# Eleven modulation chunks of a two-layer decoder trunk, moved from the expert loops into the second layer's mixing

## The chip, the cores and the metric

The kernel runs on one core of a Trainium2 chip. The metric is the time of one execution on the device in microseconds, the median of several runs. One execution was also taken by the hardware profiler. The engines are PE (matrix products), DVE and ACT (element-wise work), POOL and SP; besides their arithmetic, POOL, SP and ACT issue DMAs. Weights come from device memory (HBM) in chunks of 128 x 1024 float32, 512 KB, into on-chip memory (128 partitions).

## What is computed

A trunk of two layers over 256 tokens of width 1024. Each layer has a token mixing (convolution, windowed attention, spatial gating) and a retrieval of experts by product keys. Six modulation vectors of each layer, from one conditioning vector, shift and scale both inputs and gate both outputs:

```python
c_act = jax.nn.silu(c)
mod = (c_act @ w_ada + b_ada)[:, None, :]
sh1, sc1, g1, sh2, sc2, g2 = jnp.split(mod, 6, axis=-1)
h = rms_norm(x, norm1_g) * (1 + sc1) + sh1
proj = h @ w_in
...
x = x + g1 * (merged @ w_out)
h2 = rms_norm(x, norm2_g) * (1 + sc2) + sh2
x = x + g2 * peer_ffn(h2, peer_wq, peer_sub_keys, peer_down, peer_up)
```

In `peer_ffn` each token has 8 heads; each head takes the best 16 of 128 x 128 experts by the sum of two key scores. An expert is one row of `peer_down` (dot with h2, then gelu, times a softmax gate) and one row of `peer_up` (added with that weight).

## The kernel before

**Experts.** The first 168 tokens of layer 0 and the first 160 of layer 1 are computed densely over all 16384 experts, in two loops of 128 tiles, 128 experts each. The *down loop* (L1234 to L1329) multiplies a 512 KB tile of `peer_down` with the tokens on PE (`chunk_mm`, L357), and from some tile on makes the gates of four tokens with eight small matmuls (`gate_mm`, L1133), from one-hots that DVE compares (L1107) and ACT scales (L1117 to L1123). The gated activations `acts` fill the low part of an arena of on-chip memory, tile by tile. The *up loop* (`combine`, L1173) multiplies them with tiles of `peer_up` and adds up in PSUM.

The other 88 or 96 tokens are computed by *gathered rows*. POOL fetches 128 expert rows by an indirect DMA of 512 KB (`fetch`, L1074). DVE makes dots of the rows of `peer_down` (`dot`, L1084, in the down loop) and adds the rows of `peer_up` (`add_row`, L1099, in the up loop). PE folds the sums into PSUM at tile 125 of the up loop (`folds`, L1179). A dot or an add sets its buffer free, and only then does POOL fetch another row into it. Buffers are fixed places of the arena: among them those of early down tiles that have been used (`AHEAD_AT`).

**The picks.** The top-k work of the two token blocks on DVE is a list of pieces with costs (`fills`). Block 1 goes first, then block 0; `run_fill` runs pieces within a budget a tile. When a block's pieces are done, three transposes on PE (L934, two tiles later) bring its picks into place. Rows can be fetched from three tiles after block 1 is done (tile `begin`: 11 in layer 0, 12 in layer 1). Gates begin some tiles after both blocks' transposes. Until block 0 is done, `DOT_SLOW` dots are due in a tile; from `start` on it is `DOT_RATE`.

**The stream of chunks.** `Src.seq` lists all chunks in the order of use. Dense tiles, through a ring of 7 buffers, go alternately by ACT's and by SP's DMA queue. The *asides*, 48 chunks of `w_ada` that make the second layer's modulation, stand in the list between the tiles, at places in `ASIDES_AT` for the down loops and spread over tiles 4 to 100 of layer 0's up loop (`ASIDES_UP`). They go by SP's queue into six buffers of their own, and DVE multiplies each with `cact` and sums it (L227). The rows have POOL's queue. Each queue is served in order.

**Where the order comes from.** The expert loops run in the order in which they are written, with the decisions above taken when the program is built. The instructions of the mixing and of the other stages are ordered by a scheduler; each engine takes its own in that order. The *bridge* (L424) joins a layer's end to the next mixing: updates of X on DVE (L392), its squares' sums, the reciprocal `rn` (L376), the scaled input (L481, L487). In the mixing, chunks of `w_in` and `w_out` are split into two halves (ACT L277, DVE L270) and multiplied in three products (L359 to L361), beside attention (L606 logits, L611 to L626 softmax on DVE).

Of the kernel before, what the change touches and what calls it, by code (L numbers as in the profile page):

```python
# [14 lines left out]
OP = mybir.AluOpType  # L15
# [4 lines left out]
S = 256  # L20
DC = 8
D = 1024
# [24 lines left out]
WHERE_LAG = 3  # L47
SETS_LAG = 6
SETS_KNOWN = 22
D_FIRST = 8  # L50
DOT_SLOW = 0.3
DOT_RATE = (0.85, 0.92)
DOT_FAST = 1.6
RETIRE = 9
AHEAD_AT = (8, 12, 16, 36, 40, 44, 48, 52, 56, 60, 64, 68, 100, 28, 32)
KEPT = 100
FLUSH = 6
FIRST_LOWER = 1
AHEAD_FIRST = 4
ASIDES_AT = ((20,) * 6 + tuple(range(46, 125, 5)), (20,) * 6 + (60, 72))  # L60
ASIDES_UP = (4, 100)
F_FIRST = 4
F_LAST = 124
HELD = 2
FILL = 1.5
FILL_DOWN = (2.2, 2.1)
# [16 lines left out]
def hybrid_trunk(ctx: ExitStack, tc: tile.TileContext, x_in, c_in, vec_in, w_ada, w_in, w_out, w_pq,  # L83
# [118 lines left out]
    def dma_ahead(upto):  # L202
        while Src.loaded < min(upto, len(Src.seq)):
            kind, src, raw = Src.seq[Src.loaded]
            if kind == "aside":
                raw = stream.tile([P, D], F32, name="aside", tag=("hi", "lo")[Src.aside % 2], bufs=3)
                Src.aside += 1
            elif kind != "early":
                raw = stream.tile([P, D], F32, name="raw", tag="raw", bufs=RAW)
            if kind == "second":  # L210
                Src.later.append((Src.loaded, raw, src))
            else:
                nc.sync.dma_start(raw, src)
            raws[Src.loaded] = raw
            Src.loaded += 1
# [32 lines left out]
    def cast_step(late=None):  # L248
        k = Src.cast
        if k >= len(Src.seq):  # L250
            return False
        dma_ahead(k + 1)
        while Src.later and Src.ring[Src.later[0][0]] <= Src.ring[k + 1] - 1 + RAW - QUEUE_LAG:
            nc.scalar.dma_start(*Src.later.pop(0)[1:])
        kind, _, arg = Src.seq[k]
        raw = raws.pop(k)
        Src.cast += 1
        if kind == "aside":
            Src.asides.append((k, lambda: ada_chunk(arg[0], arg[1], raw)))
        elif kind == "ada":  # L260
            ada_chunk(arg[0], arg[1], raw)
        elif kind in ("whole", "early", "second"):
            ready.append((raw, None))
        else:
            hi = stream.tile([P, D], F32R, name="hi", tag="hi", bufs=3)
            lo = stream.tile([P, D], F32R, name="lo", tag="lo", bufs=3)

            def low():
                if arg is None:
                    nc.vector.tensor_sub(lo, raw, hi.bitcast(F32))  # L270
                else:
                    nc.vector.scalar_tensor_tensor(lo, raw, arg, hi.bitcast(F32), op0=OP.mult,
                                                   op1=OP.subtract)

            with tc.high_priority(offset=AHEAD):
                if arg is None:
                    nc.scalar.copy(hi, raw)  # L277
                else:
                    nc.scalar.activation(hi, raw, AF.Copy, scale=arg)
                if late is None:  # L280
                    low()
                else:
                    late.append(low)
            ready.append((hi, lo))
        load_more(k)
        return True
# [16 lines left out]
    def ada(layer, groups, kind="ada"):  # L303
        return [(kind, w_ada[layer, p], (layer, p)) for g in groups for p in range(8 * g, 8 * g + 8)]
# [11 lines left out]
    def mats(src, layer, n, kind="mat"):  # L316
        return [(kind, src[layer, p], None) for p in range(n)]

    seq = []
    for layer in range(DEPTH):  # L320
        body = [("whole" if n in WHOLE_IN[layer] else "mat", w_in[layer, n], None) for n in range(16)]
# [2 lines left out]
        if layer == 0:  # L324
# [6 lines left out]
            body = head + body[n:]  # L331
            body = first[:2] + body[:n] + first[2:] + mix(body[n:], ada(0, [2, 3, 4]))
        body += mix(tail[:6], ada(0, [5])) + tail[6:] if layer == 0 else tail
        seq += body + [("whole" if n in WHOLE_PQ else "mat", w_pq[layer, n], None) for n in range(16)]
        dn, un = ([t if n % 2 else ("second", *t[1:]) for n, t in enumerate(mats(w, layer, 128, "whole"))]
                  for w in (down, up))
        for n, at in enumerate(AHEAD_AT):
            dn[AHEAD_FIRST + n] = ("early", dn[AHEAD_FIRST + n][1], region(at * S, D))
        aside = ada(1, [0, 1, 2, 3, 4] if layer + 1 < DEPTH else [5], "aside")
        for n, at in reversed(tuple(enumerate(ASIDES_AT[layer]))):  # L340
            dn.insert(at, aside[n])
        if layer + 1 < DEPTH:
# [3 lines left out]
    Src.seq = seq  # L346
    for t in seq:
        Src.ring.append(Src.ring[-1] + was if Src.ring else 0)
        was = t[0] not in ("early", "aside")
    Src.ring.append(Src.ring[-1] + was)  # L350
    dma_ahead(RAW)

# [655 lines left out]
    def experts(layer, rest):  # L1008
# [225 lines left out]
        for i in range(128):  # L1234
# [32 lines left out]
                known_to[0] = SETS[0][1]  # L1267
                fetch()
            if start is None:
                run_fill(FILL_DOWN[layer] if begin is None else FILL_DOWN[layer] - 1.2 * DOT_SLOW)  # L1270
            if known:
                known_at.append((i + PICKS_LAG, known.pop()))
                if begin is None:
# [25 lines left out]
                for row in [row for row in free if any(row is r for r in passing)]:  # L1299
                    free.remove(row)  # L1300
            n = i - AHEAD_FIRST
            if 0 <= n < len(AHEAD_AT) and AHEAD_AT[n] >= 28:
                assert not retired
                free.append(region(AHEAD_AT[n] * S, D))
                if AHEAD_AT[n] != KEPT:
                    passing.append(free[-1])
                fetch()
# [130 lines left out]
```

## Time and profile before

| | us |
|---|---|
| median of 3 runs | 1582.73 (1582.06 to 1584.29) |
| profiled execution | 1584.51, span 1582.6 |
| layer 0: mixing and queries | 0 to 188.85 |
| layer 0: down loop, up loop | 188.85 to 509.46, to 823.6 |
| layer 1: mixing and queries | 823.6 to 976.9 |
| layer 1: down loop, up loop | 976.9 to 1285.8, to the end |

The stages' borders are read from PE's timeline. In the rows that follow, an instruction is named by engine and line, with output and inputs. A bracket such as `[3.54 <-DMA raw<-in_up]` is the time for which the engine stood before it, and what ended that. A group's row has its count, busy time and mean, then idle time and what ended most of it. `raw` is the ring of dense tiles, `arena` the big on-chip memory in which row buffers lie too, `spots` the dots' inputs, the sums and three more row buffers.

### The profile page before, as it was taken

The numbers are of one execution on the slowest core, as the hardware profiler recorded it, in microseconds if no ns is written. First come the engines' busy times: TensorE is split into PE (matmuls) and PEld (weight loads), VectorE is DVE, ScalarE is ACT, GpSimd is POOL, SyncE is SP. The second block draws the span as 40 slices with busy tenths as digits, with TensorE's granted clock in tenths as the row PEclk, the third lists the DMA queues.
The fourth block names the chain that finished last, engine by engine and source line by source line (L and its number), as shares of the span: only waits on it lengthen the run. The fifth ranks groups of instructions, "written<-read, shape, count | busy, mean of one in ns | idle before, by whom it ended". The sixth has DMA issues, their size and how long they took to land.

```text
span 1582.6 us, 28957 instructions
## 1 busy us (share of the span) xinstructions
PE 1542.3 (97%) x11240; PEld 1505.1 (95%) x11240; DVE 1000.0 (63%) x2255; ACT 472.5 (30%) x1356; POOL 496.8 (31%) x424
## 2 busy tenths in 40 slices
PE   6999999999999999998999999999999999999997
PEld 5879999999999999998999899999999999999997
DVE  6778898677787444444337578877667754444434
ACT  2346313465553000000026663134656610000000
POOL 1000124334344434444200001245443334444441
PEclk9999999999999999999999999999999999999998
DMA  9998489999999999999955574899999999999995
GB/s 385 339 375 319 138 289 348 418 418 419 417 418 416 415 419 419 418 419 419 412 189 171 186 258 139 292 351 419 417 418 419 418 419 419 418 419 419 419 418 211
DMA packets 156681, 571.21 MB, mean 361 GB/s; under 512 B 18131, under 2 KB 18659, under 8 KB 155392
## 3 DMA queue, kind: packets, MB, share of 16 engines
q1 hardware_dynamic: 66096, 241.07, 39.7%
q0 software_dynamic: 55744, 202.36, 32.0%
q10 hardware_dynamic: 34704, 125.93, 19.9%
q8 instruction: 88, 1.44, 0.3%
q14 instruction: 49, 0.40, 0.1%
HBM read 564.02 MB, written 4.09 MB: 359 GB/s over the span
## 4 chain that ended last, share of the span: by engine, by line
PE 40%; DMA 38%; issue 8%; DVE 7%; POOL 4%; ACT 2%; ACTq 0%; POOLq 0%; SPq 0%; DVEq 0%
DMA arena<-in_up,arena 17%; PE acc L1173 17%; DMA arena<-in_down_rows,arena 12%; PE ch L357 9%; DMA spots<-in_down_rows,arena 3%; DMA raw<-in_up 3%; POOL arena L1074 3%; PE ch L359 2%; PE ch L360 2%; PE ch L361 2%; DVE raw L227 1%; DMA raw<-in_w_ada 1%; PE ch L446 1%; DVE arena L1084 1%; PE g L952 1%
## 5 line engine op out<-in xcount | busy, mean ns | idle before, releaser
L1173 PE MATMUL acc<-arena,raw 128*128 128x168 f32 (+1 forms) x4096 | 580.5, 305 | 9.0 <-DMA raw<-in_up 9.0
L1173 PEld LDWEIGHTS acc<-arena,raw 128*128 128x128 f32 x4096 | 577.6, 192 | 11.3 <-DMA raw<-in_up 11.2
L357 PE MATMUL ch<-arena,raw 128*128 128x168 f32 (+2 forms) x3776 | 560.7, 307 | 0.1
L357 PEld LDWEIGHTS ch<-arena,raw 128*128 128x128 f32 x3776 | 536.2, 190 | 5.6 <-issue 1.8
L1099 DVE SCALAR_TENSOR_TENSOR spots<-arena,spots 128x1024 f32<-128x1024 f32 x156 | 200.4, 1284 | 222.1 <-DMA arena<-in_up,arena 220.8
L1074 POOL DMA_INDIRECT arena<-in_up,arena x159 | 215.1, 1353 | 280.5 <-DMA arena<-in_up,arena 203.9
L1074 POOL DMA_INDIRECT arena<-in_down_rows,arena x151 | 178.3, 1181 | 242.9 <-DVE arena L1084 180.7
L1084 DVE SCALAR_TENSOR_TENSOR arena<-arena,spots 128x1024 f32<-128x1024 f32 x151 | 183.1, 1222 | 86.1 <-DMA arena<-in_down_rows,arena 79.6
L1117 ACT ACTIVATE arena<-arena,parts 128x128 f16<-128x128 f16 x164 | 64.6, 394 | 142.1 <-DVE arena L1107 102.5
L388 ACT ACT_TABLE_LOAD x6 | 7.7, 1283 | 284.9 <-PE acc L1173 284.8
L357 PE MATMUL ch<-arena 128*128 128x160 f32 (+2 forms) x544 | 86.0, 317 | 6.1 <-issue 3.6
L357 PEld LDWEIGHTS ch<-arena 128*128 128x128 f32 x544 | 79.8, 192 | 11.2 <-ACT arena L410 5.2
L1150 ACT ACTIVATE arena<-ch 128x336 f32<-128x336 f32 (+32 forms) x122 | 41.9, 343 | 149.4 <-PE ch L357 128.9
L227 DVE SCALAR_TENSOR_TENSOR aside<-aside,arena 128x1024 f32<-128x1024 f32 x48 | 58.6, 1220 | 43.9 <-DMA aside<-in_w_ada 43.8
L359 PE MATMUL ch<-hh,hi 128*128 128x256 f32 x288 | 82.6, 289 | 2.0 <-DVE arena L477 1.9
L360 PE MATMUL ch<-hh,lo 128*128 128x256 f32 x288 | 81.8, 284 | 0.0
L361 PE MATMUL ch<-hh,hi 128*128 128x256 f32 x288 | 81.7, 284 | 0.0
L270 DVE TENSOR_TENSOR lo<-raw,hi 128x1024 fp32r<-128x1024 f32 x42 | 51.2, 1225 | 37.3 <-ACT hi L277 36.3
L227 DVE SCALAR_TENSOR_TENSOR raw<-raw,arena 128x1024 f32<-128x1024 f32 x48 | 57.9, 1217 | 8.9 <-DMA raw<-in_w_ada 5.4
L1119 ACT ACTIVATE arena<-arena,parts 128x128 f16<-128x128 f16 x164 | 63.4, 387 | 0.0
L1123 ACT ACTIVATE arena<-arena,parts 128x128 f16<-128x128 f16 x164 | 63.4, 386 | 0.0
L1121 ACT ACTIVATE arena<-arena,parts 128x128 f16<-128x128 f16 x164 | 63.4, 386 | 0.0
(231 smaller groups left out, 1661.9 us busy)
## 6 DMA issues: line engine op xcount, KB each, us to landing
raw<-in_up SPq DMA_DIRECT2D x128, 512.0 KB
raw<-in_up ACTq DMA_DIRECT2D x128, 512.0 KB
raw<-in_down SPq DMA_DIRECT2D x114, 512.0 KB
raw<-in_down ACTq DMA_DIRECT2D x112, 512.0 KB
raw<-in_w_ada SPq DMA_DIRECT2D x48, 512.0 KB
aside<-in_w_ada SPq DMA_DIRECT2D x48, 512.0 KB
raw<-in_w_pq SPq DMA_DIRECT2D x32, 512.0 KB
arena<-in_down SPq DMA_DIRECT2D x30, 512.0 KB
```

Source lines behind the costliest of these rows:

```text
L227: nc.vector.scalar_tensor_tensor(raw, raw, 1.0, cact, op0=OP.mult, op1=OP.mult, accum_out=mods[layer][:, col:col + 1])
L357: nc.tensor.matmul(dst, hi[:, cols], k[0], start=start, stop=stop, **kw)
L359: nc.tensor.matmul(dst, hi[:, cols], k[0], start=start, stop=False, **kw)
L360: nc.tensor.matmul(dst, lo[:, cols], k[0], start=False, stop=False, **kw)
L361: nc.tensor.matmul(dst, hi[:, cols], k[1], start=False, stop=stop, **kw)
L1074: nc.gpsimd.indirect_dma_start(out=held[n], out_offset=None, in_=rows if n >= TS else down_rows[:, :], in_offset=bass.IndirectOffsetOnAxis ...
L1084: nc.vector.scalar_tensor_tensor(row, row, 1.0, R_DX[which(k)[0]], op0=OP.mult, op1=OP.mult, accum_out=R_DOTS[:, k:k + 1])
L1099: nc.vector.scalar_tensor_tensor(R_SUM[s], row, w, R_SUM[s], op0=OP.mult, op1=OP.add)
L1117: nc.scalar.activation(og[0][:, 0, i, :], oh[:, 0, i, :], AF.Copy, scale=parts[:, 0, t + i:t + i + 1])
L1119: nc.scalar.activation(og[1][:, 0, i, :], oh[:, 0, i, :], AF.Copy, scale=parts[:, 1, t + i:t + i + 1])
L1121: nc.scalar.activation(og[0][:, 1, i, :], oh[:, 1, i, :], AF.Copy, scale=parts[:, 0, t + 2 + i:t + 3 + i])
L1173: nc.tensor.matmul(acc[d // 2][:, (d % 2) * S:(d % 2) * S + T], u[:, d * P:(d + 1) * P], acts[:, i, :], start=i == 0 and d % 2 == 0, stop= ...
```

## The change

The 11 chunks are columns 24 to 31 (the second layer's second shift, `sh2`) and 40 to 42 (of its last gate, `g2`). They are no asides any more. A new kind of chunk, `inline`, loads them by POOL's DMA queue into named places of the arena, and DVE multiplies them there:

```diff
+MIXED = ((24, 10, 76), (25, 10, 80), (26, 10, 84), (27, 11, 29), (28, 11, 33), (29, 11, 37), (30, 11, 41), (31, 14, 17), (40, 19, 45), (41, 20, 49), (42, 22, 17))
...
-            if kind == "aside":
+            if kind == "inline":
+                raw = raw[0]
+                nc.gpsimd.dma_start(raw, src)
+            elif kind == "aside":
...
+        if kind == "inline":
+            view = (lambda v: v.rearrange("p (a b) -> p a b", a=2)) if len(raw.shape) == 3 else (lambda v: v)
+            nc.vector.scalar_tensor_tensor(raw, raw, 1.0, view(cact), op0=OP.mult, op1=OP.mult,
+                                           accum_out=mods[arg[1]][:, arg[2]:arg[2] + 1])
+            ada_end(arg[1], arg[2], 8)
...
+    def beside(layer, n):
+        return [mixed(col, at) for col, m, at in MIXED if layer == 1 and m == n]
...
+        body = [t for n, b in enumerate(body) for t in [b] + beside(layer, n)]
...
+        aside = [t for t in aside if t[2][1] not in apart]
```

Each entry is a column, the chunk of the second mixing's list behind which it stands, and a place in units of 256 columns. The asides left are 18 in layer 0's down loop (22 before), 14 in its up loop (18), and 5 in layer 1's down loop (8). With this go the pace of the dots, the row buffers and the picks' budget:

```diff
-D_FIRST = 8
-DOT_SLOW = 0.3
+D_FIRST = 7
+DOT_SLOW = 0.9
...
-RETIRE = 9
+RETIRE = 4
...
-ASIDES_AT = ((20,) * 6 + tuple(range(46, 125, 5)), (20,) * 6 + (60, 72))
+ASIDES_AT = ((20,) * 6 + tuple(range(46, 125, 7)), (20,) * 5)
...
-                run_fill(FILL_DOWN[layer] if begin is None else FILL_DOWN[layer] - 1.2 * DOT_SLOW)
+                if begin is None or i < begin + D_FIRST:
+                    run_fill(FILL_DOWN[layer])
+                elif fills[0]:
+                    run_fill(FILL_DOWN[layer] - 1.2 * DOT_SLOW)
+                else:
+                    run_aside()
...
-            if 0 <= n < len(AHEAD_AT) and AHEAD_AT[n] >= 28:
+            if 0 <= n < len(AHEAD_AT) and AHEAD_AT[n] >= 36:
```

`D_FIRST` is the tile after `begin` from which dots are due. `RETIRE` is the number of pieces left at which the passing row buffers are given up. The last line takes two places (28 and 32) from the row buffers.

How the order moves is shown at three places. The first is the end of the picks in layer 1's down loop. On PE, L357 (L379 of the changed kernel) is the dense tiles' matmul, eight a tile, and L934 (L956) the transposes of the picks; L1133 (L1155) is the first gate. Before:

```order
L1035 MATMUL g<-ident,arena 96x128 x8
L357 MATMUL ch<-arena,raw 128x160 x8
L357 MATMUL ch<-arena 128x160 x88
L934 MATMUL g<-ident,arena 128x128 x3
L357 MATMUL ch<-arena 128x160 x32
L357 MATMUL ch<-arena,raw 128x160 x128
L934 MATMUL g<-ident,arena 128x128 x3
L357 MATMUL ch<-arena,raw 128x160 x64
L1133 LDWEIGHTS arena
```

and in the changed kernel:

```order
L1057 MATMUL g<-ident,arena 96x128 x8
L379 MATMUL ch<-arena,raw 128x160 x8
L379 MATMUL ch<-arena 128x160 x88
L956 MATMUL g<-ident,arena 128x128 x3
L379 MATMUL ch<-arena 128x160 x32
L379 MATMUL ch<-arena,raw 128x160 x184
L956 MATMUL g<-ident,arena 128x128 x3
L379 MATMUL ch<-arena,raw 128x160 x72
L1155 LDWEIGHTS arena
```

The second transposes stand behind 7 more tiles (184 - 128 = 56 matmuls), at tile 41 for 34, and the first gate one tile more, at 50 for 42. In layer 0 the same count moves the second transposes from tile 32 to 38. On DVE at that place, L1084 (L1106) is a dot, L902 to L912 (L924 to L934) match picks, L922 to L924 (L944 to L946) make the softmax gate that the transposes need. Before:

```order
L902 TENSOR_TENSOR arena<-arena,iota_87 128x2048
L907 TENSOR_TENSOR arena<-arena 128x2048
L911 TENSOR_TENSOR arena<-arena 128x8x128
L911 TENSOR_TENSOR arena<-arena 128x8x64
L911 TENSOR_TENSOR arena<-arena 128x8x32
L912 TENSOR_TENSOR arena<-arena 128x128
L1084 SCALAR_TENSOR_TENSOR arena<-arena,spots 128x1024
L922 TENSOR_REDUCE arena<-arena 128x8
L923 RECIPROCAL arena<-arena 128x8
L924 TENSOR_TENSOR arena<-arena 128x128
L1084 SCALAR_TENSOR_TENSOR arena<-arena,spots 128x1024 x3
```

and in the changed kernel:

```order
L929 TENSOR_TENSOR arena<-arena 128x2048
L1106 SCALAR_TENSOR_TENSOR spots,arena<-spots 128x1024
L1106 SCALAR_TENSOR_TENSOR arena<-arena,spots 128x1024
L933 TENSOR_TENSOR arena<-arena 128x8x128
L933 TENSOR_TENSOR arena<-arena 128x8x64
L933 TENSOR_TENSOR arena<-arena 128x8x32
L934 TENSOR_TENSOR arena<-arena 128x128
L1106 SCALAR_TENSOR_TENSOR arena<-arena,spots 128x1024 x2
L944 TENSOR_REDUCE arena<-arena 128x8
L945 RECIPROCAL arena<-arena 128x8
L946 TENSOR_TENSOR arena<-arena 128x128
L1106 SCALAR_TENSOR_TENSOR arena<-arena,spots 128x1024
```

Dots stand between the pieces: 18 ahead of the gate in layer 1 now (3 before), 16 in layer 0.

The second place is DVE's part of the bridge from layer 0 to layer 1's mixing; L264 of the changed kernel is an inline chunk's product. Before:

```order
L270 TENSOR_TENSOR lo<-raw,hi 128x1024
L392 SCALAR_TENSOR_TENSOR arena<-acc,mod_111,arena 128x256 x8
L439 TENSOR_TENSOR arena<-arena 128x256 x2
L442 TENSOR_TENSOR arena<-arena 128x256 x6
L270 TENSOR_TENSOR lo<-raw,hi 128x1024
L376 RECIPROCAL rn<-rn 128x2
L481 TENSOR_TENSOR arena<-arena,g 128x512 x2
L487 SCALAR_TENSOR_TENSOR hh<-arena,mod_112,hh 128x256 x2
```

and in the changed kernel:

```order
L264 SCALAR_TENSOR_TENSOR arena,mod_112<-arena 128x1024
L279 TENSOR_TENSOR lo<-raw,hi 128x1024
L414 SCALAR_TENSOR_TENSOR arena<-acc,mod_111,arena 128x256 x8
L461 TENSOR_TENSOR arena<-arena 128x256 x2
L464 TENSOR_TENSOR arena<-arena 128x256 x6
L279 TENSOR_TENSOR lo<-raw,hi 128x1024
L264 SCALAR_TENSOR_TENSOR arena,mod_112<-arena 128x1024
L398 RECIPROCAL rn<-rn 128x2
L264 SCALAR_TENSOR_TENSOR arena,mod_112<-arena 128x1024
L503 TENSOR_TENSOR arena<-arena,g 128x512 x2
```

The products of columns 24, 25 and 26 stand before the updates, before the reciprocal, and before the scaling of the input. The third place is POOL's queue in layer 0's up loop, where L1096 is a fetched row and L208 an inline chunk's load; in the changed kernel it reads:

```order
L1096 DMA arena<-in_up,arena 128x1024 x6
L208 DMA arena<-in_w_ada 128x1024
L1096 DMA arena<-in_up,arena 128x1024 x3
L1096 DMA spots<-in_up,arena 128x1024
L1096 DMA arena<-in_up,arena 128x1024 x2
L208 DMA arena<-in_w_ada 128x1024
L1096 DMA arena<-in_up,arena 128x1024 x7
```

Columns 27 and 28 are loaded behind the 50th and the 56th row, where before rows alone stood; the other nine loads come behind the loop's last row. The products of these two stand on DVE behind the 46th and 47th add.

More of the change, by code (lines that the diff above doesn't have):

```diff
@@ L211, in dma_ahead @@
                 Src.later.append((Src.loaded, raw, src))
-            else:
+            elif kind != "inline":
                 nc.sync.dma_start(raw, src)
@@ L257, in cast_step @@
         Src.cast += 1
-        if kind == "aside":
+        if kind == "inline":
[3 more added lines that the diff above has]
+            ada_end(arg[1], arg[2], 8)
+        elif kind == "aside":
             Src.asides.append((k, lambda: ada_chunk(arg[0], arg[1], raw)))
@@ L317, in mats, with mixed @@
         return [(kind, src[layer, p], None) for p in range(n)]
+    def mixed(col, at):
+        if at == 90:
+            raw = region(at * S, 2 * D).rearrange("p (a b) -> p a b", a=2)[:, :, :D // 2]
+        else:
+            raw = region(at * S, D)
+        return ("inline", w_ada[1, col], (raw, 1, col))
+    def beside(layer, n):
+        return [mixed(col, at) for col, m, at in MIXED if layer == 1 and m == n]
+    apart = [col for col, _, _ in MIXED]
     seq = []
@@ L348, in hybrid_trunk @@
         Src.ring.append(Src.ring[-1] + was if Src.ring else 0)
-        was = t[0] not in ("early", "aside")
+        was = t[0] not in ("early", "aside", "inline")
     Src.ring.append(Src.ring[-1] + was)
@@ L1269, in experts @@
             if start is None:
-                run_fill(FILL_DOWN[layer] if begin is None else FILL_DOWN[layer] - 1.2 * DOT_SLOW)
+                if begin is None or i < begin + D_FIRST:
+                    run_fill(FILL_DOWN[layer])
+                elif fills[0]:
+                    run_fill(FILL_DOWN[layer] - 1.2 * DOT_SLOW)
+                else:
+                    run_aside()
             if known:
```

## The prediction

> **What bounds the kernel now.** I read the page's head and its slices first, then the busy time by stage, then the waits of PE and of DVE in the stages that the change touches. From the page:
>
> ```profile
> span 1582.6 us, 28957 instructions
> PE 1542.3 (97%) x11240; PEld 1505.1 (95%) x11240; DVE 1000.0 (63%) x2255; ACT 472.5 (30%) x1356; POOL 496.8 (31%) x424
> ...
> L1173 PE MATMUL acc<-arena,raw 128*128 128x168 f32 (+1 forms) x4096 | 580.5, 305 | 9.0 <-DMA raw<-in_up 9.0
> ...
> L1084 DVE SCALAR_TENSOR_TENSOR arena<-arena,spots 128x1024 f32<-128x1024 f32 x151 | 183.1, 1222 | 86.1 <-DMA arena<-in_down_rows,arena 79.6
> ```
>
> PE is busy 97% of the span, so only PE's waits, its slow clock, and work that pushes it back can move the end. The stages, from the windows table (stretch; busy us and instructions of PE, PEld, DVE, ACT, POOL; granted clock; DMA share; GB/s):
>
> ```profile
> 188.85:268.70 79.85, 78.14 (x549) 77.43 (x548) 68.16 (x319) 15.99 (x30) 28.21 (x32) 1.00 0.84 292
> 509.46:674.00 164.54, 164.53 (x1154) 164.06 (x1153) 79.80 (x78) 0.45 (x1) 68.45 (x53) 1.00 1.03 418
> 674.00:787.00 113.00, 104.68 (x704) 103.37 (x703) 48.52 (x47) 0.00 (x0) 41.32 (x32) 0.97 1.03 419
> 823.60:880.00 56.40, 56.31 (x436) 54.15 (x436) 42.11 (x91) 37.88 (x90) 0.00 (x0) 1.00 0.58 187
> 1057.40:1285.80 228.40, 226.23 (x1814) 223.18 (x1813) 165.52 (x313) 125.67 (x450) 94.49 (x85) 0.99 1.03 418
> 1285.80:1560.00 274.20, 273.52 (x2011) 273.04 (x2011) 119.06 (x97) 0.72 (x2) 125.12 (x90) 1.00 1.02 417
> ```
>
> The row at 509.46 is the first part of layer 0's up loop, that at 674 its end; 823.6 to 880 is the start of layer 1's mixing; the last two are layer 1's down loop after its picks, and its up loop. In the expert loops the DMA engines are full at 418 GB/s; in the mixing they are not (187). A chunk of 512 KB costs 524288 B / 418 GB/s = 1.254 us of a full DMA. PE loses time to that only at the end of layer 0's up loop. Its rows there in the timeline (start, us, wait in brackets), the chain's last full-speed stretch before, and the windows table at the largest wait:
>
> ```profile
> 682.17 9.39 PE L1173 MATMUL acc<-arena,raw 128*128 128x168 f32 x64 [1.03 <-DMA raw<-in_up]
> 692.11 8.11 PE L1173 MATMUL acc<-arena,raw 128*128 128x168 f32 x55 [0.56 <-DMA raw<-in_up]
> ...
> 734.75 8.78 PE L1173 MATMUL acc<-arena,raw 128*128 128x168 f32 x48 [3.54 <-DMA raw<-in_up]
> 744.26 4.83 PE L1173 MATMUL acc<-arena,raw 128*128 128x168 f32 x32 [0.73 <-DMA raw<-in_up]
> 751.54 18.76 PE L1173 MATMUL acc<-arena,raw 128*128 128x168 f32 x118 [2.46 <-DMA raw<-in_up]
> ...
> 509.63 157.55 PE acc L1173 x1104
> ...
> 730.00:740.00 10.00, 6.46 (x34) 6.20 (x33) 4.82 (x6) 0.00 (x0) 4.16 (x3) 0.83 1.03 415
> ```
>
> 157.55 us / 1104 = 142.7 ns an instruction, 2.283 us a tile of 16. The 126 tiles ahead of the folds would take 287.7 us; they take 810.33 - 509.46 = 300.9 (the fold's row is quoted below). So 13.1 us are lost: 8.3 in the five waits shown, the rest in a clock of 0.83 and smaller gaps. Layer 1's up loop loses nothing (273.52 of 274.20).
>
> **The change, part by part.**
>
> *Fewer chunks in the full stretches.* The 11 chunks leave SP's queue: 4 in layer 0's down loop, 4 in its up loop, 3 in layer 1's down loop. Two come back among layer 0's up rows (order, in the change section). Net 6 chunks x 1.254 = 7.5 us of DMA in layer 0, 3 x 1.254 = 3.8 in layer 1. In layer 0 this acts on the 13.1 us lost. Bounds: only the chunks' own time, 7.5, or all 13.1. I take all of it, since the lost time is the waits of `raw<-in_up`, and the up loop's SP queue, which carries those loads, has 14 chunks spread over tiles 4 to 100 where it had 18. Bringing 13.1 us through a relief of 7.5 needs slack elsewhere: there is some, because any wait that PE gains earlier (next item) also gives the DMA time. **-13.1.**
>
> *Dots of 0.9 a tile, picks later.* Before, 16 rows are fetched, then POOL waits for a buffer until the second picks are out; dots read rows as follows (POOL, DVE, PE timelines of layer 0):
>
> ```profile
> 256.27 1.08 POOL L1074 DMA_INDIRECT arena<-in_down_rows,arena  x1 [0.65 <-issue]
> 270.76 1.14 POOL L1074 DMA_INDIRECT arena<-in_down_rows,arena  x1 [13.40 <-DVE parts L943]
> ...
> 268.70 0.49 PE L934 MATMUL g<-ident,arena 128*128 128x128 f32 x3
> ...
> 283.09 1.22 DVE L1084 SCALAR_TENSOR_TENSOR arena<-arena,spots 128x1024 f32<-128x1024 f32 x1 [1.78 <-DMA arena<-in_down_rows,arena]
> ...
> 493.10 4.62 PE ch L357 x32
> ...
> 810.33 6.58 PE L1179 MATMUL acc<-fold,spots 128*128 128x64 f32 x48
> ```
>
> Row 283.09 is the 16th dot, and it started when its row landed. The second transposes (268.70, after tile 32's matmuls) stand after tile 38's in the changed order: 268.70 + 6 x 2.31 = 282.5 (the chain's row of two tiles: 4.62 / 2 = 2.31). In the changed order 16 dots stand on DVE before the sums that the transposes need, so they can't come before 283.1 + 1.2 for the dot + 1.2 (an estimate) for the gate's three small operations and the hand-over = 285.5: PE waits 3.0, and its clock drops after it. The price of that is the row of 730 to 740: 0.17 x 10 us = 1.7 after a wait of 3.54. Bounds: 0 (the row lands earlier) to 4.7. **+4.7. Layer 0 together: -8.4.** The Trainium skill, "TensorE: Matmul & The Clock Gate", section "HAM oscillation", has the clock fall to half only when PE idles over some 3.4 us. By that a wait of 3.0 would cost no clock and layer 0 would give -10.1; the row of 1080 below shows the clock fall after 1.30 and 0.65, so I go by the rows.
>
> In layer 1 the same (PE and DVE timelines, and the windows table from 1080):
>
> ```profile
> 1057.41 0.49 PE L934 MATMUL g<-ident,arena 128*128 128x128 f32 x3
> 1057.74 17.55 PE L357 MATMUL ch<-arena,raw 128*128 128x160 f32 x128
> ...
> 1086.32 0.52 PE L1133 MATMUL g<-arena 128*128 128x128 f16 x2 [1.30 <-ACT arena L1117]
> 1087.48 1.16 PE L1133 MATMUL g<-arena 128*128 128x128 f16 x6 [0.65 <-ACT arena L1117]
> ...
> 1066.38 1.23 DVE L1084 SCALAR_TENSOR_TENSOR arena<-arena,spots 128x1024 f32<-128x1024 f32 x1 [0.25 <-DMA arena<-in_down_rows,arena]
> ...
> 1081.18 1.22 DVE L1084 SCALAR_TENSOR_TENSOR arena<-arena,spots 128x1024 f32<-128x1024 f32 x1 [1.74 <-DMA arena<-in_down_rows,arena]
> 1083.69 1.22 DVE L1084 SCALAR_TENSOR_TENSOR arena<-arena,spots 128x1024 f32<-128x1024 f32 x1 [1.28 <-DMA arena<-in_down_rows,arena]
> ...
> 1080.00:1090.00 10.00, 7.99 (x56) 7.06 (x54) 7.54 (x15) 3.15 (x11) 5.17 (x5) 0.87 1.03 421
> ...
> 1565.67 6.61 PE L1179 MATMUL acc<-fold,spots 128*128 128x32 f32 x30 [4.51 <-DVE spots L1099]
> ```
>
> The transposes move from tile 34 to 41 in the order: 1057.4 + 7 x 2.194 = 1072.8 (17.55 / 8 = 2.194). Eighteen dots stand before them, and the 18th row landed at 1081.18, so sums at 1083.7: PE waits 10.9 if rows land as before, 0 if they come 11 us sooner. They may come sooner, since while PE stands its loads stop once the ring is full, and the rows have the DMA for themselves. I take the middle, 5.4, plus 1.7 of clock. Against this go the gates' waits of 1086 (1.30 + 0.65, and 0.13 x 10 us of clock: 3.3), as there are no gates before tile 50 now. PE's own path in layer 1 thus grows by 3.8. But at the end PE waited 4.51 us for the rows' sum (the last row above), and the rows' path is now 3 chunks, 3.8 us, shorter. The end is the later of the two: PE's 3.8 - 4.5 = -0.7, the rows' -3.8. **Layer 1's loops: -0.7**, bounds -3.8 and +4.8 (10.9 + 1.7 - 3.3 - 4.5).
>
> *Products in the mixing.* Nine chunks are loaded and multiplied while layer 1's mixing runs. PE, DVE and group rows:
>
> ```profile
> 823.56 4.50 PE L446 MATMUL ch<-arena,raw 128*128 128x257 f32 x20
> ...
> 829.18 0.17 DVE L376 RECIPROCAL rn<-rn 128x2 f32<-128x2 f32 x1 [0.73 <-ACT rn L375]
> 830.30 1.28 DVE L481 TENSOR_TENSOR arena<-arena,g 128x512 f32<-128x512 f32 x2 [0.96 <-PE g L382]
> ...
> L227 DVE SCALAR_TENSOR_TENSOR aside<-aside,arena 128x1024 f32<-128x1024 f32 x48 | 58.6, 1220 | 43.9 <-DMA aside<-in_w_ada 43.8
> ```
>
> A product is 1.22 us, with its accumulator's read 1.30. Columns 25 and 26 go to places that the last `acts` hold until PE ends the up loop (823.6); only then POOL issues them, and their products stand on DVE ahead of the reciprocal (829.18) and ahead of L481 (830.30), on which PE waits. At the mixing's 187 GB/s a chunk takes 2.8 us, two 5.6: they land at about 829.2 + issue, the second product ends near 832.5, and L481 is some 2.5 late. The Trainium skill, "DMA: Bandwidth & Descriptors", section "Anatomy of one DMA", gives about 2.0 us fixed and bytes / 436 GB/s, an estimate of 3.2 us for one chunk; with it the first lands at 828 and the sum would be 1.5 lower. Of the other seven, two or three lie in the softmax, where DVE is dense (42.11 of 56.40 busy from 823.6); PE has chunks of `w_in` to do meanwhile. I take 1.5. **+4.0**, bounds 0 and 11 x 1.30 = 14.3.
>
> *The two among layer 0's up rows.* Their products stand after up-adds 46 and 47 on DVE, and their loads behind the 50th and 56th row on POOL's queue, so DVE stands until these land (POOL and DVE timelines):
>
> ```profile
> 642.61 1.35 POOL L1074 DMA_INDIRECT arena<-in_up,arena  x1 [2.11 <-DMA arena<-in_up,arena]
> ...
> 704.62 1.28 DVE L1099 SCALAR_TENSOR_TENSOR spots<-arena,spots 128x1024 f32<-128x1024 f32 x1 [2.47 <-DMA arena<-in_up,arena]
> ```
>
> The 50th row was issued at 642.61 and added at about 704: some 17 rows, 60 us, are under way. DVE then stands for nine rows, about 30 us, with landed rows piling up; the queue does not run dry, and adds of 1.28 us catch up. Nothing; if the cover failed, rows would be late at the folds.
>
> **The sum**: -8.4 + 4.0 - 0.7 = -5.1. The profiled execution took 1584.5, so 1579.4; it lies 1.8 above the median 1582.73, so the forecast of the median is **1577.6 us**.
>
> **Rivals.**
> *Full relief.* Rows land early enough that no transposes wait: layer 0 -13.1, layer 1 -3.8, mixing +1.5: -15.4, 1567.3 us. For it: room in the DMA ahead of the picks (a share of 0.84 from 188.85); against it: the 16th row was issued at 256.27, before dots held anything up, and still took until 283.
> *Layer 1's picks at the old landing.* The wait is the full 10.9, layer 1 +4.8: -8.4 + 4.0 + 4.8 = +0.4, 1583.1: no difference. For it: each dot quoted above waited for its row.
> *Slower: rows pace the gates.* Before, dots are 10 of some 17 landed rows when gates begin; after, 23 or 24, all that landed. Compares stand on DVE behind 0.92 dots a tile. From 1066.38 to 1083.69 six rows took 17.31, 2.89 each: 0.92 x 2.89 = 2.66 us a tile, while PE needs 228.40 / 94 = 2.43. If that lasts for half of the 73 tiles from 43 to 116, PE loses 36 x 0.23 = 8.4 on top of the full wait: +0.4 + 8.4 = +8.8, 1591.5. It decides from 2.43 / 0.92 = 2.64 us a row. Against it: rows came faster later on, else the down loop (226.23 of 228.40) would have waited.
> *Products on the path.* All 14.3 us reach PE in the mixing: -8.4 + 14.3 - 0.7 = +5.2, 1587.9. Against it: PE has other work for most.
>
> **How the numbers follow.** Forecast 0.44 (its own range -3.2 to -10), full relief 0.13, old landing 0.22, rows pace 0.14, products 0.07. A measurement tells 0.2%, 3.2 us, from no change. Faster 0.44 + 0.13 = 0.57; within it 0.22; slower 0.21. From 1567 to 1588 the range leaves out the rows' pace and half of the full relief, 0.20.
>
> **What would show it.** Right: `raw<-in_up` waits at 680 to 755 gone; PE waiting 2 to 5 us ahead of the second transposes in layer 0 and 3 to 11 in layer 1; 1 to 3 us ahead of the bridge's first products; the wait ahead of layer 1's folds gone or short. Wrong: up-loop waits that stay, gates that wait tile after tile in layer 1, or an attention tail that is several us longer.

## The result, and the profile after

The changed kernel takes 1601.51 us (median of 4 runs, 1599.54 to 1603.77) against 1583.09 for the kernel before, measured beside it: a ratio of 1.0117, 95% interval 1.0099 to 1.0134. It is slower by 18.4 us, where 1577.6 was forecast and the range ended at 1588. Its profiled execution took 1599.54, span 1597.8, so 15.2 us of span more than before. A few executions of three of the versions below ran from 6% longer to 3.5 times as long; the times and ratios here leave them out. By stages of PE's timeline (the first row of each stage in both traces):

| stage | before | after | difference | forecast |
|---|---|---|---|---|
| layer 0 down loop | 320.6 | 332.8 | +12.2 | +4.7 |
| layer 0 up loop, to the folds | 300.9 | 292.7 | -8.2 | -13.1 |
| folds and last tiles | 13.2 | 13.2 | 0 | 0 |
| layer 1 mixing and queries | 153.3 | 159.0 | +5.7 | +4.0 |
| layer 1 down loop | 308.9 | 323.7 | +14.8 | +3.8 |
| layer 1 up loop, to the folds | 275.1 | 275.5 | +0.4 | 0 |
| layer 1 folds and last tiles | 17.5 | 8.1 | -9.4 | -4.5 |

Both down loops are some 13 us longer, +27.0 together where the prediction had +8.5. The page of the changed kernel, its head and the DMA's rate in 40 slices of 39.9 us:

```profile
span 1597.8 us, 28958 instructions
...
PE 1543.1 (97%) x11240; PEld 1505.3 (94%) x11240; DVE 996.5 (62%) x2248; ACT 471.1 (29%) x1353; POOL 497.1 (31%) x435
...
GB/s 386 344 366 326 142 281 364 416 416 417 413 415 283 377 419 419 418 400 418 419 264 221 198 257 138 275 332 394 418 418 419 418 340 417 419 419 419 419 419 257
```

PE's work is the same (1543.1 for 1542.3). The DMA is no longer full at the end of either down loop: 283 and 377 GB/s in the slices from 479 us, 340 in that from 1278, where the same slices of before stood at 415 or more. The waits view of PE (operation, what it waited for: us in total, times, longest):

```profile
PE g L956 <- DVE arena L934: 7.6, 1, 7.6
PE ch L379 <- ACT arena L1172: 5.3, 1, 5.3
...
PE g L956 <- DVE arena L946: 4.2, 2, 2.6
PE g L1155 <- ACT arena L1139: 3.7, 5, 0.9
PE acc L1195 <- DMA raw<-in_up: 2.9, 2, 2.0
```

`raw<-in_up` has fallen from 9.0 to 2.9 us. In its place stand waits for DVE's picks (L934, L946) and for ACT.

**Layer 1's picks.** Timelines of DVE and PE, then PE's clock there (windows: PE, PEld, DVE, ACT, POOL busy; clock; DMA share; GB/s):

```profile
1048.99 1.22 DVE L1106 SCALAR_TENSOR_TENSOR arena<-arena,spots 128x1024 f32<-128x1024 f32 x1
1065.55 1.22 DVE L1106 SCALAR_TENSOR_TENSOR arena<-arena,spots 128x1024 f32<-128x1024 f32 x1 [15.33 <-DMA arena<-in_down_rows,arena]
1066.70 1.22 DVE L924 TENSOR_TENSOR arena<-arena,iota 128x2048 f16<-128x2048 f16 x1
1067.95 2.29 DVE L929 TENSOR_TENSOR arena<-arena 128x2048 f16<-128x2048 f16 x1
...
1084.77 0.27 PE L956 MATMUL g<-ident,arena 128*128 128x128 f32 x1
1092.63 0.48 PE L956 MATMUL g<-ident,arena 128*128 128x128 f32 x1 [7.59 <-DVE arena L934]
1095.68 0.47 PE L956 MATMUL g<-ident,arena 128*128 128x128 f32 x1 [2.57 <-DVE arena L946]
...
1084.80:1096.00 11.20, 1.04 (x5) 0.51 (x4) 9.61 (x19) 0.44 (x1) 6.97 (x5) 0.66 1.01 402
```

The eighth dot ends at 1050. The ninth row isn't there, and DVE stands 15.33 us, with both match pieces (L924 to L934, L924 again) behind it in its order. When the row comes, the pieces and nine more dots follow, with another 7.0 us of waits for rows among them (the longest 2.28). PE has reached the transposes at 1084.8 and waits 10.2 us; in that time DVE is busy 9.61 us of 11.20, and the DMA still moves 402 GB/s. Why the ninth row is late stands on POOL and in the chain:

```profile
1027.06 0.94 POOL L1096 DMA_INDIRECT arena<-in_down_rows,arena  x1 [0.31 <-issue]
1028.00 0.60 POOL L1072 DMA_DIRECT2D pair_in<-chosen  x1
...
1040.41 1.41 POOL L1078 DMA_DIRECT2D pairs<-pair_in  x2 [11.27 <-issue]
1041.81 0.68 POOL L1081 DMA_DIRECT2D spots<-dot_in  x1
1042.80 1.02 POOL L1096 DMA_INDIRECT arena<-in_down_rows,arena  x1 [0.30 <-issue]
...
1028.00 9.50 DMA pair_in<-chosen
...
1041.81 20.23 DMA spots<-dot_in
```

After eight rows POOL writes picks and tokens for the other row sets to memory (`spread_rest`) and reads them back. That write queues behind the eight rows, POOL stands for it, and the ninth row is issued only at 1042.80, behind `spots<-dot_in`, which takes 20.23 us. The kernel before had the same gap, from the eighth row to the ninth:

```profile
1017.69 0.94 POOL L1074 DMA_INDIRECT arena<-in_down_rows,arena  x1 [0.30 <-issue]
...
1028.15 1.41 POOL L1056 DMA_DIRECT2D pairs<-pair_in  x2 [8.39 <-DMA pair_in<-chosen]
...
1032.68 1.98 POOL L1074 DMA_INDIRECT arena<-in_down_rows,arena  x1 [2.46 <-issue]
```

There 3 dots instead of 18 stood ahead of the gate, so nobody waited.

**Layer 0's first gates.** DVE, ACT and PE timelines, and the clock:

```profile
283.63 0.33 PE L956 MATMUL g<-ident,arena 128*128 128x128 f32 x1 [1.67 <-DVE arena L946]
...
294.71 1.28 DVE L1129 TENSOR_TENSOR arena<-iota,picks 128x1024 f16<-128x1024 f16 x2
...
295.49 0.40 ACT L1139 ACTIVATE arena<-arena,parts 128x128 f16<-128x128 f16 x1 [8.76 <-DVE arena L1129]
...
300.66 10.06 PE L379 MATMUL ch<-arena,raw 128*128 128x168 f32 x48 [5.29 <-ACT arena L1172]
...
286.00:306.00 20.00, 14.71 (x85) 14.45 (x84) 16.09 (x28) 5.90 (x19) 8.81 (x7) 0.85 1.03 418
```

The transposes themselves waited 1.67 us. The picks were in place at 285, but ahead of the first compares (L1129) stand five dots and three asides on DVE: eight operations of 1.22 us, and two of the dots waited another 0.79 and 0.88 us for rows. ACT's factors (L1139) stand 8.76 us for the compares; behind them on ACT is the gelu of two dense tiles (L1172), without which PE has no free PSUM bank: 5.29 us, and a clock of 0.85 for 20 us.

**The end of the loops.** Windows of the changed kernel at the end of layer 0's down loop, PE's waits in its up loop, and windows over the last folds, of the kernel before and of the changed one:

```profile
480.00:515.00 35.00, 33.29 (x264) 32.02 (x263) 17.09 (x32) 20.86 (x78) 4.06 (x4) 1.00 0.87 315
...
749.47 6.50 PE L1195 MATMUL acc<-arena,raw 128*128 128x168 f32 x32 [2.00 <-DMA raw<-in_up]
756.92 57.27 PE L1195 MATMUL acc<-arena,raw 128*128 128x168 f32 x400 [0.94 <-DMA raw<-in_up]
```

```profile
1560.80:1578.40 17.60, 13.05 (x66) 12.67 (x64) 7.33 (x11) 0.00 (x0) 0.00 (x0) 0.71 0.08 31
```

```profile
1585.40:1593.50 8.10, 8.10 (x66) 7.87 (x64) 2.63 (x6) 0.00 (x0) 0.00 (x0) 1.00 0.05 20
```

The last dot now stands 35 us ahead of the end of layer 0's down loop, where it stood 7 before. So the row buffers hold rows for the up loop that no one can add yet, and POOL stands (4.06 us busy of 35) while the DMA has room. Layer 1's rows come in time for the folds: 66 matrix products take 8.1 us for 17.6. The wait was only 4.51 of that difference of 9.4; for the rest PE was busy, 13.05 us for work that now takes 8.10, at a clock of 0.71 for 1.00.

### The profile page after: what moved, and what is told of

It reads as the page before. It is cut to its first block, busy times and chain, and to the rows that moved or that the text cites. A ratio compares the mean times of both kernels' runs of the same rounds, so it can differ in the third digit from the quotient of the medians.

```text
span 1597.8 us, 28958 instructions
## 1 busy us (share of the span) xinstructions
PE 1543.1 (97%) x11240; PEld 1505.3 (94%) x11240; DVE 996.5 (62%) x2248; ACT 471.1 (29%) x1353; POOL 497.1 (31%) x435
## 5 line engine op out<-in xcount | busy, mean ns | idle before, releaser
L379 PE MATMUL ch<-arena,raw 128*128 128x168 f32 (+2 forms) x3776 | 566.0, 309 | 5.9 <-ACT arena L1172 5.3
L379 PEld LDWEIGHTS ch<-arena,raw 128*128 128x128 f32 x3776 | 541.3, 192 | 11.9 <-ACT arena L1172 5.5
L1096 POOL DMA_INDIRECT arena<-in_up,arena x159 | 207.0, 1302 | 323.4 <-DMA arena<-in_up,arena 138.6
L1096 POOL DMA_INDIRECT arena<-in_down_rows,arena x153 | 182.2, 1191 | 219.9 <-DVE arena L1106 142.0
L1106 DVE SCALAR_TENSOR_TENSOR arena<-arena,spots 128x1024 f32<-128x1024 f32 x153 | 185.1, 1222 | 65.5 <-DMA arena<-in_down_rows,arena 56.8
L1172 ACT ACTIVATE arena<-ch 128x320 f32<-128x320 f32 (+39 forms) x126 | 44.8, 356 | 249.8 <-PE ch L379 220.8
L1165 DVE SCALAR_TENSOR_TENSOR arena<-arena,g 128x200 f32<-128x200 f32 (+20 forms) x82 | 42.5, 519 | 87.5 <-ACT arena L1163 81.4
L379 PE MATMUL ch<-arena 128*128 128x160 f32 (+2 forms) x544 | 87.6, 321 | 5.7 <-issue 3.4
L379 PEld LDWEIGHTS ch<-arena 128*128 128x128 f32 x544 | 81.4, 195 | 10.6 <-ACT arena L432 4.6
L1139 ACT ACTIVATE arena<-arena,parts 128x128 f16<-128x128 f16 x164 | 64.8, 395 | 70.7 <-DVE arena L1129 52.4
L231 DVE SCALAR_TENSOR_TENSOR aside<-aside,arena 128x1024 f32<-128x1024 f32 x37 | 45.2, 1220 | 56.3 <-DMA aside<-in_w_ada 56.3
```

The costliest lines, as they stand in the source:

```text
L231: nc.vector.scalar_tensor_tensor(raw, raw, 1.0, cact, op0=OP.mult, op1=OP.mult, accum_out=mods[layer][:, col:col + 1])
L379: nc.tensor.matmul(dst, hi[:, cols], k[0], start=start, stop=stop, **kw)
L1096: nc.gpsimd.indirect_dma_start(out=held[n], out_offset=None, in_=rows if n >= TS else down_rows[:, :], in_offset=bass.IndirectOffsetOnAxis ...
L1106: nc.vector.scalar_tensor_tensor(row, row, 1.0, R_DX[which(k)[0]], op0=OP.mult, op1=OP.mult, accum_out=R_DOTS[:, k:k + 1])
L1139: nc.scalar.activation(og[0][:, 0, i, :], oh[:, 0, i, :], AF.Copy, scale=parts[:, 0, t + i:t + i + 1])
```

## The experiments

All were run beside the kernel before; a stage's length is read as in the table above.

**The pace alone.** All 48 chunks stay asides; only the pace, the budget and the row buffers change:

```diff
-D_FIRST = 8
-DOT_SLOW = 0.3
+D_FIRST = 7
+DOT_SLOW = 0.9
...
-RETIRE = 9
+RETIRE = 4
```

> The kernel before with the new pace alone (0.9 dots a tile from the seventh tile after the first block, the new budget of the picks, two row buffers fewer); all 48 chunks stay asides. Theory A, the pace is what costs: DVE stands for rows ahead of the second block's gate, so PE waits some 10 us at layer 1's second transposes as in the changed kernel, and the median lies 9 to 20 us above before, 1592 to 1603. Theory B, the inline chunks cost: within 3 us of before, 1580 to 1586, and no wait at the transposes over 3 us.

Measured: 1601.88 us, ratio 1.0112 (1.0091 to 1.0133). The down loops are 334.8 and 323.9 us, +14.2 and +15.0; the mixing is 153.3, as before. PE at the second transposes of both layers:

```profile
286.99 0.48 PE L934 MATMUL g<-ident,arena 128*128 128x128 f32 x1 [4.24 <-DVE arena L924]
...
1091.42 0.48 PE L934 MATMUL g<-ident,arena 128*128 128x128 f32 x1 [4.99 <-DVE arena L912]
1095.53 0.48 PE L934 MATMUL g<-ident,arena 128*128 128x128 f32 x1 [3.63 <-DVE arena L924]
```

The new pace, with the budget and buffers that go with it, brings the whole loss within the intervals (1.0112 for 1.0117).

**The chunks alone**, with the old pace:

```diff
-D_FIRST = 7
-DOT_SLOW = 0.9
+D_FIRST = 8
+DOT_SLOW = 0.3
...
-RETIRE = 4
+RETIRE = 9
```

> The changed kernel with the old pace (0.3 dots a tile, old budget, old row buffers): only the 11 chunks are moved. Theory A: the mixing is some 6 us longer as in the changed kernel, but the loops gain from 9 chunks less, so 1573 to 1581 and no wait over 3 us at the transposes. Theory B: slower than before by 10 to 18, 1593 to 1601.

Measured: 1581.04 us, ratio 0.9984 (0.9972 to 0.9996), at the upper end of what theory A expected. Layer 0's up loop is 292.4 us (-8.5) and the mixing 159.1 (+5.8): the gain is mostly given back there. Layer 0's folds and last tiles take 16.6 us for 13.2: PE waits 1.54 us ahead of these folds, right behind the last add of layer 0's rows, so with a faster up loop the rows are the later path. Layer 1's folds still wait 5.2 us. Pace and chunks add up: +17.7 and -2.5 of ratio 1.0112 and 0.9984 make 15, and the changed kernel has 18.4, within the intervals.

**Half the pace** in the changed kernel (`DOT_SLOW = 0.5`):

> The changed kernel with 0.5 instead of 0.9 dots a tile until the gates: 6 dots instead of 16 or 18 stand ahead of the second block's gate, and these rows had landed long before. Theory A: the waits at the second transposes are under 1 us, and the time comes back by 12 us or more, to 1573 to 1588. Theory B: 1597 to 1602, as the changed kernel.

Measured: 1578.76 us, ratio 0.9966 (0.9951 to 0.9981): some 23 us less than the changed kernel by the change of one constant, and less than before. So the dots a tile (with the part of the picks' budget that hangs on them) make the loss, and not the chunks or the buffers. The second transposes have no wait. Gates begin at the old tile in layer 1 and two tiles later than that in layer 0. In layer 1 two waits at the gates stay, the larger of them:

```profile
1061.09 0.49 PE L956 MATMUL g<-ident,arena 128*128 128x128 f32 x3
...
1093.88 0.58 PE L1155 MATMUL g<-arena 128*128 128x128 f16 x2 [3.12 <-ACT arena L1139]
```

**Asides later.** In the changed kernel the asides of tile 20 move to later tiles:

```diff
-ASIDES_AT = ((20,) * 6 + tuple(range(46, 125, 7)), (20,) * 5)
+ASIDES_AT = (tuple(range(48, 120, 4)), (60, 72, 84, 96, 108))
```

> The changed kernel with the six and five asides of tile 20 spread over later tiles of the down loops, so that fewer transfers stand beside the first rows. Theory A: the 18th row lands 3 to 6 us earlier, layer 1's wait at the second transposes falls from 10.2 to 4 to 7 us, layer 0's likewise, and the median is 1590 to 1597. Theory B: 1599 to 1603, unchanged, since nothing of the mixing changes.

Measured: 1608.26 us, ratio 1.0158 (1.0135 to 1.0181). A miss for both theories: DVE's wait for the ninth row is 15.40 us, unchanged, that at layer 1's transposes 9.3, and the down loops are 336.9 and 329.2 us, longer than with the asides early; why they are longer is open. Fewer transfers beside the first rows do not bring the ninth sooner, so what holds it lies elsewhere.

**No asides before the gates.** The changed kernel without its new `else: run_aside()`:

> The changed kernel without the new branch that runs asides between the picks' last piece and the gates' start. In the changed kernel three such products stand on DVE ahead of layer 0's first compares, ACT's factors wait for these, and a dense tile's gelu behind them on ACT holds PE for 5.3 us. Theory A1, all that DVE has ahead of the compares counts: this wait falls to 1 to 3 us and the median by 2 to 5, to 1597 to 1600. Theory A2, only the rows' landing counts: the dots wait anyway, and the median stays at 1600 to 1603.

Measured: 1598.59 us, ratio 1.0087 (1.0063 to 1.0112). The wait of PE for the gelu falls from 5.29 to 3.34 us:

```profile
301.38 9.99 PE L379 MATMUL ch<-arena,raw 128*128 128x168 f32 x48 [3.34 <-ACT arena L1172]
```

This is near the 1 to 3 us that theory A1 had for the wait. The time, some 3 us less, is what A1 expected too, but the two intervals overlap.

**The early spread.** In the changed kernel `SETS_LAG = 2` for 6: the transfers of `spread_rest` are issued ahead of the first rows.

> The changed kernel with the transfers that spread picks and tokens for the other row sets issued four tiles earlier, ahead of the first rows instead of behind eight of them, so that POOL doesn't stand for them while rows are due. Theory A3, the 9th row comes late because POOL stands between the 8th and the 9th: layer 1's wait of DVE for the 9th row (15.3 us) falls under 6, the wait at the second transposes from 10.2 to under 5, and the median to 1588 to 1597. Theory A4, rows are paced by their share of the DMA: the 18th row lands as before, the wait at the transposes stays at 8 to 11, and the median at 1599 to 1603.

Its time is that of one execution alone, 1599.68 us, the profiled one, so it carries no interval. The waits are read from its profile. The longest wait of DVE for a row ahead of the gate, and PE at the second transposes of layer 1:

```profile
1047.78 1.23 DVE L1106 SCALAR_TENSOR_TENSOR arena<-arena,spots 128x1024 f32<-128x1024 f32 x1 [2.30 <-DMA arena<-in_down_rows,arena]
...
1077.59 0.33 PE L956 MATMUL g<-ident,arena 128*128 128x128 f32 x1 [1.35 <-DVE arena L934]
1082.25 0.48 PE L956 MATMUL g<-ident,arena 128*128 128x128 f32 x1 [4.34 <-DVE arena L946]
```

15.33 has become 2.30: POOL's stand between the eighth and the ninth row is shown as the cause of DVE's long wait, theory A3. Of PE's 10.2 us at the transposes 5.7 stay, more than A3's 5, so the late ninth row is less than half of that wait; the rest stays with the dots ahead and their other rows. Layer 0's down loop is 326.4 us (332.8), layer 1's 319.1 (323.7). The median that A3 expected did not come: layer 1's up loop is 285.2 us, 10 longer, with a clock of 0.83 in its first 30 us and eight short waits of PE, 4.1 us in all, for which the profile names nothing that ended them ("issue"). Why the up loop begins so is open.

**The bridge freed.** With 0.5 dots a tile, columns 25 and 26 become asides of layer 0's down loop again:

```diff
-MIXED = ((24, 10, 76), (25, 10, 80), (26, 10, 84), (27, 11, 29),
+MIXED = ((24, 10, 76), (27, 11, 29),
...
-ASIDES_AT = ((20,) * 6 + tuple(range(46, 125, 7)), (20,) * 5)
+ASIDES_AT = ((20,) * 6 + tuple(range(46, 125, 6)), (20,) * 5)
```

> The kernel with 0.5 dots a tile and nine chunks moved instead of eleven: columns 25 and 26, whose products stand in the bridge, are asides of layer 0's down loop again. If the two products make the mixing longer, the stage between the bridge and layer 1's down loop (158.9 us with eleven, 153.3 before) falls to 155 to 157, and layer 0's loops grow by up to 2.5 us of DMA, so 1575 to 1580 in all. If the other products in the softmax do, the mixing stays within 1 us of 158.9 and the median is 1579 to 1582.

Measured: 1576.38 us, ratio 0.9952 (0.9932 to 0.9971). The mixing is 156.3 us, 2.6 less, and layer 0's loops are no longer (321.6 and 292.3 for 322.8 and 292.8).

**The early spread with half the pace**:

> The kernel with 0.5 dots a tile, with the early spread of the other row sets. Theory A3: rows 9 and later land 5 us or more earlier, the waits at layer 1's gates (1.8 and 3.1 us) go, and the median is 1573 to 1578. Theory A4: as with 0.5 dots alone, 1577 to 1581.

Measured: 1579.55 us, ratio 0.9957 (0.9921 to 0.9994), inside theory A4's range, but not for its reason: layer 0's down loop is 316.0 us (322.8), layer 1's 312.0 (315.4), and layer 1's up loop 280.4 (273.8). The gates' waits in layer 1 stay (1.87 and 3.10). The start of layer 1's up loop:

```profile
1282.00:1310.00 28.00, 25.17 (x160) 24.22 (x159) 21.93 (x18) 0.44 (x1) 18.68 (x17) 0.88 1.02 410
```

**The old pace with the bridge freed**, `DOT_SLOW = 0.3` and the old budget and buffers with nine chunks moved:

> Nine chunks moved (25 and 26 stay asides of layer 0), with the old pace of 0.3. If 0.5 dots a tile gained anything by itself, this is slower than the same kernel with 0.5 (1576.4) by 2 us or more, 1578.5 to 1582, since the sum of layer 1's rows is late at the folds again (5.2 us of wait with 0.3). If pace matters only by the waits that 0.9 brings, it is within 1.5 us: 1575 to 1578.

Measured: 1579.97 us, ratio 0.9977 (0.9962 to 0.9992); 0.5 is some 3.6 us better, though the two intervals overlap. The down loops are shorter with 0.3 (317.4 and 311.0 us for 321.6 and 316.7), but the rows are late at the folds: waits of 2.5 us in layer 0 and 3.2 in layer 1, none with 0.5.

**The softmax freed.** Columns 40 and 41 asides of layer 1 again, on top of the freed bridge:

```diff
-(31, 14, 17), (40, 19, 45), (41, 20, 49), (42, 22, 17))
+(31, 14, 17), (42, 22, 17))
...
-(20,) * 5)
+(20,) * 5 + (60, 72))
```

> The kernel with 0.5 dots a tile and nine chunks, with columns 40 and 41 asides of layer 1's down loop again, so that their products don't stand in the softmax. If these two hold the attention's tail, the mixing (156.3 us with nine, 153.3 before) falls to 153 to 155 and the median to 1573 to 1576, less up to 2.5 given back by the two chunks in layer 1. If not, the mixing stays at 156 to 156.5 and the median at 1576 to 1579.

Measured: 1580.21 us, ratio 0.9987 (0.9968 to 1.0007). A miss: the mixing is 158.1 us, longer, with a new wait of 2.8 us in the attention, perhaps since the scheduler places the rest anew, which is not shown. What the softmax products cost by themselves stays open.

**Late picks alone.** The kernel before, with the second block's transposes six tiles later, and 0.8 dots a tile between the picks' last piece and the gates:

```diff
-DOT_FAST = 1.6
+DOT_FAST = 0.8
...
-                known_at.append((i + PICKS_LAG, known.pop()))
+                known_at.append((i + (PICKS_LAG if begin is None else 8), known.pop()))
```

> The kernel before with the second block's transposes six tiles later and nothing else moved: all asides, 0.3 dots a tile, and after the picks 0.8, so that 10 rows, all landed, stand ahead of the first compares. Gates then start where the changed kernel has them, with the same last tile. Theory A, DVE standing for rows is what costs: no wait over 2 us at the transposes and the gates' start, only denser gates at the loops' ends: 1583 to 1591. Rival theory C, gates that start eight tiles later cost as such: each down loop 8 us longer or more and the median 1597 to 1605.

Measured: 1587.96 us, ratio 1.0032 (1.0022 to 1.0043), within theory A's range. The first gates stand six tiles later in both layers here, where the changed kernel has six in layer 0 and eight in layer 1. So later gates by themselves cost some 5 of the 18 us, not the 16 or more of theory C. No profile shows where the 5 us are, and A's "no wait over 2 us" is not shown.

**The early spread in layer 0 alone**, with half the pace and the bridge freed:

```diff
-                if i == begin + SETS_LAG:
+                if i == begin + (2 if layer == 0 else SETS_LAG):
```

> The kernel with 0.5 dots a tile and nine chunks, with the early spread in layer 0 alone. With the early spread in both layers layer 0's down loop was 316.0 us for 322.8, but layer 1's up loop 280.4 for 273.8. If these two belong to the layer where the spread is early, this takes the gain without the loss: layer 0's down loop 315 to 318, layer 1's up loop 273 to 275, the median 1569 to 1573. If not, 1575 to 1579.

Measured: 1569.49 us, ratio 0.9913 (0.9896 to 0.9929), as expected: layer 0's down loop 316.0 us, layer 1's up loop 273.9. This is the fastest version of the study, 13.6 us under the kernel before. Against the freed bridge, layer 0's down loop is 5.6 us shorter, and most of that lies where the first rows are fetched, not at the gate. (Layer 1's, where nothing was changed, is 3.8 us shorter too, 312.9 for 316.7; why is open.) Windows of the freed bridge and of this version:

```profile
222.00:262.00 40.00, 37.13 (x247) 36.59 (x246) 36.29 (x145) 7.28 (x15) 22.57 (x24) 0.96 0.94 311
```

```profile
222.00:262.00 40.00, 40.00 (x283) 40.00 (x283) 38.28 (x151) 7.74 (x16) 22.39 (x20) 1.00 1.00 355
```

PE's waits there (0.70 and 1.04 us of "issue", 1.13 for a dense tile) and the fall of its clock are gone. Why is not shown. The version still has a wait like that of layer 0's first gates, in layer 1:

```profile
1063.35 1.97 PE L379 MATMUL ch<-arena,raw 128*128 128x160 f32 x6 [5.69 <-ACT arena L1172]
```

## Why the prediction was wrong, point by point

*Fewer chunks, -13.1.* Measured -8.2 in the changed kernel, -8.5 with the chunks alone. The lower bound, the chunks' own 7.5 us of DMA, was the better size. Waits of 2.9 us stay. The DMA's loss ahead of the up loop cost little: with the chunks alone it moves 416 GB/s there, and the gain is the same.

*Where it failed.* The step that failed is the price of "Dots of 0.9 a tile, picks later": +4.7 in layer 0's down loop and +3.8 in layer 1's, 8.5 in all. Measured were +12.2 and +14.8, 27.0 in all. The working asked when the last row ahead of the transposes lands and stopped there.

*Layer 0's picks, +4.7.* The transposes' wait was forecast as 3.0 and was 1.67. The loss came ten microseconds later, at the first compares, behind dots and asides on DVE and through ACT's order on PE: 5.29 and the clock. The prediction asked only who stands ahead of the gate, not who stands ahead of the next thing that PE needs from DVE. Two waits at the loop's last gates, 0.89 and 0.64, are new too. The loop lost 12.2.

*Layer 1's loops, -0.7.* Here the step reads: "They may come sooner, since while PE stands its loads stop once the ring is full, and the rows have the DMA for themselves. I take the middle, 5.4". The wait was 10.2, next to the upper bound of 10.9. The rows did not come sooner but later: the 16th was there 103.4 us after the loop's start (DVE's row at 1089.62), for 98.4 before (1075.28). When PE began to stand, 14 of the 18 dots were done or under way, and the DMA stayed full (402 GB/s). DVE had by then stood 15.33 us for the ninth row, with match work behind it, and for four later rows. The trace of before showed POOL held up between the eighth and the ninth row (the spread's stand there), and the working priced only the last row of the 18. Denser gates had no term either: the five waits for ACT's factors in the view above (L1139, 3.7 us) all stand at the ends of the two down loops. The late picks alone cost 5 us over both layers, though no profile shows that this is where. Layer 1's loops together: +14.8 + 0.4 - 9.4 = +5.8 for -0.7. What the wait at the folds costs was underpriced too: 9.4 for 4.5, by the clock. This error went the other way and hid part of the loss.

*The mixing, +4.0.* Measured +5.7, with 2.6 of it from the two products in the bridge (forecast 2.5), which the freed bridge shows. The two chunks landed 5.7 and 7.2 us after their issue (at 827.74 and 828.28); the 3.2 us for one chunk that the prediction sets beside its own estimate was too short here. The other part is the attention's waits of 1.77 and 1.39 us for ACT (L657), forecast as 1.5; that the products on DVE cause these is argued, since the softmax freed did not settle it. The bridge's mechanism was right, the attention's size too low.

*The two among layer 0's up rows, nothing.* Right in effect by a narrow margin, and a number was misread. DVE stood 38.6 us for them (timeline):

```profile
677.33 1.23 DVE L264 SCALAR_TENSOR_TENSOR arena<-arena 128x1024 f32<-128x1024 f32 x1 [16.21 <-DMA arena<-in_w_ada]
...
702.18 1.23 DVE L264 SCALAR_TENSOR_TENSOR arena<-arena 128x1024 f32<-128x1024 f32 x1 [22.42 <-DMA arena<-in_w_ada]
```

The first was issued at 650.49 and landed 27 us later; so seven or eight rows are under way, not the 17 of the prediction. In the kernel before, the 50th row is added at 668.77; the add at 704.62 that was quoted is the 60th row's, issued at 676.47. The queue did stop: POOL stood 25 us for a free buffer, until 706. The rows came back just in time, with the last add done 0.9 us ahead of the folds. The folds waited in two other versions, 1.54 us with the chunks alone and 1.66 without the early asides.

*The rivals.* "Layer 1's picks at the old landing" named the right place; with it the sum was +0.4, since the other terms were too good. "Rows pace the gates" had the right sign and the wrong mechanism: from the first gate at 1116.8 until the last tiles of the loop they run without a wait.

*The clock.* In layer 0 of the changed kernel the clock was 0.85 over the 20 us around the wait of 5.29 us. In the kernel before it was 0.87 in the stretch of 1080, after waits of 1.30 and 0.65, and 0.70 at layer 0's folds, where PE did not wait at all:

```profile
812.00:823.50 11.50, 11.50 (x66) 11.50 (x66) 3.38 (x7) 3.92 (x10) 0.00 (x0) 0.70 0.25 85
```

The rule that the prediction quotes from the Trainium skill, "TensorE: Matmul & The Clock Gate", section "HAM oscillation", of idle time over some 3.4 us, fits the first of these and not the other two.

## What to carry to other kernels

When work is put ahead of something urgent on an in-order engine, price the arrival of each of its inputs, from the first one that is late, and not the last one alone; what is queued behind a stand is late by that much, whatever its own inputs. Follow the order one engine further: a late compare on DVE stopped factors on ACT, and a gelu behind them stopped PE. A transfer that must read back what it wrote is worth trying ahead of the bulk loads in its queue instead of behind eight of them: moved there in layer 0, it took 1576.4 us to 1569.5. Moved in both layers, it gained nothing (1578.8 and 1579.6), so such a move has to be measured layer by layer.

## What the runs showed of the hardware

A wait of PE can cost more than its length: 4.51 us ahead of the last folds were 9.4 us of time, at a clock of 0.71 against 1.00. It need not: behind the 10.2 us at layer 1's transposes the clock was 0.68 for 4 us (1096 to 1100), 1.3 us of time. On POOL's queue an issue waits in this program until the eighth transfer before it has landed: the trace shows its transfers using eight completion semaphores in turn, each issue waiting for the last user of its own. That is how the program was built, and whether the chip itself has such a limit is not shown. The issue at 1062.81 waits for the transfer of 1041.81, with seven rows between them:

```profile
1062.81 0.93 POOL L1096 DMA_INDIRECT arena<-in_down_rows,arena  x1 [10.45 <-DMA spots<-dot_in]
```
